# Due times of a list schedule shifted label by label, in a two-block transformer kernel

## Chip, cores and metric
One core of a Trainium2 chip runs the kernel. The metric is the device time of one execution in microseconds (us), the median of several runs; less is better.

## What is computed
Two transformer blocks, one behind the other, on 256 tokens of width 1024 in float32. The first puts 16 meta tokens in front, and has grouped-query attention (8 heads on 2 key and value heads, part A), differential attention (4 heads, two score maps each, part B), an output projection and a SwiGLU feed-forward of width 2816. The second has a gated spatial branch, a dilated window attention in three patterns, two gates, a merge through two branch matrices and an output matrix, and a squared-relu feed-forward of width 4096. In short:

```python
h = rms_norm(x, attn_norm_g)
proj = einsum('bld,de->ble', h, w_in)             # q, k, v of A and of B
out_a = softmax(qa ka^T * scale) va               # after norm and rope of q and k
out_b = rms_norm((p0 - lam * p1) vb) * 0.8        # p0, p1 = two softmaxes per head
x = x + concat(out_a, out_b) @ w_out
h = rms_norm(x, ffn_norm_g)
x = x + (silu(h @ w_gate) * (h @ w_up)) @ w_down
...
merged = g_a * (y_a @ w_branch_a) + g_b * (y_b @ w_branch_b)   # second block
h = h + rms_norm(merged @ w_out)
h = h + rms_norm(square(relu(rms_norm(h) @ w_up)) @ w_down)
```

## The kernel before
All weights come as 235 chunks of 128 x 1024 float32 through four raw buffers (wraw). Each chunk is split into a high part (whi, ScalarE rounds it to fp32r) and a low part (wlo, VectorE subtracts), into one of six pairs of buffers; a product is then the sum of three fp32r matmuls, high by high, high by low and low by high. Activations are held the same way (hx for the normed input, mix for what goes into output projections). Results come in eight PSUM banks, each read by ScalarE and VectorE before it is used again.

No engine call is issued where it stands in the code. A `Recorder` (line 235) takes each one down with its dependences, its price by a formula (`price`, line 308; a VectorE operation costs 68 + 1.042 ns per column, for one) and the label that is current then. The labels name stages: for the first block PqA0 to PvB3 (projections), K1 and K2 (norm of a key), Q1 (norm sums of a query), V1 (transposed values), SA and SB (scores and softmax), TA and TB (transposed probabilities), VA and VB (times the values), N1 and N2 (norm of B), WO (output projection), "sums" and "warm" at the start, gateA and upA (the first 512 columns of the feed-forward by tokens), lead and f4 to f21 (the rest of it in columns of 128); for the second block names with a quote: GV, GU, SP (spatial branch), AV (values), Pq and Pk (projections), S2, T2, V2 (attention), GT (gates), BR (the two branch products and their merge), and out2, mlp0, mlp1, lead2, m4 to m31, down2 without one. `transposed` adds t0 and t1 to a label for its two groups of transposes.

`flush` is called twice (lines 1152 and 1461): behind f6, and at the end. Each call turns the recorded operations into an order. It sets a target end for every matmul, takes the due time of every other operation back from those through prices and latencies, and runs a list scheduler (`schedule`, line 346) in which each engine, whenever it is free, takes what is ready in the plan and due first. It does that six times; each round's targets are the PE times of the round before, with BIAS, a fixed -3 us on twelve labels of transposes. The order with the least PE clock in the plan is issued. Operations of one score group (R.group) are kept together, and buffers and banks are given out when an operation is recorded, ahead of any order. SP issues all DMAs in the scheduled order too.

Of the kernel before, what the change touches and what calls it, by code (L numbers as in the profile page):

```python
# [29 lines left out]
class Plan:  # L30


    def __init__(self):
        self.tasks = {}
# [164 lines left out]
def _within(a, b):  # L199
# [13 lines left out]

LATE = {
    ("tensor", "scalar"): 240.0, ("tensor", "vector"): 250.0, ("tensor", "tensor"): 0.0,
    ("scalar", "tensor"): 280.0, ("scalar", "vector"): 145.0, ("scalar", "scalar"): 0.0, ("scalar", "gpsimd"): 220.0,
# [8 lines left out]
def late(a, b):  # L227
    return LAND if a == "sync" else LATE.get((a, b), 150.0)

# [5 lines left out]
class Recorder:  # L235


    def __init__(self, tc, nc):
        self.tc, self.nc = tc, nc
        self.ops, self.acc, self.label, self.next = [], {}, "", set()  # L240
        self.clock = {e: 0.0 for e in ("tensor", "vector", "scalar", "gpsimd", "sync")}

    def engine(self, name):
# [160 lines left out]
    def flush(self):  # L404
        ops = self.ops
        pe, target = self.clock["tensor"], []
        for o in ops:
            if o.eng == "tensor":
                pe += o.cost
            target.append(pe if o.eng == "tensor" else 1e18)  # L410
        best = None
        for _ in range(ROUNDS):
            target = [t + BIAS.get(o.label, 0.0) for t, o in zip(target, ops)]
            order, at, clock = self.schedule(target)
            if best is None or clock["tensor"] < best[2]["tensor"]:
                best = order, at, clock
            target = [at[o.i] + o.cost if o.eng == "tensor" else 1e18 for o in ops]
        order, at, self.clock = best
        for i in order:
            o = ops[i]  # L420
            o.at = at[i]
            o.fn(*o.args, **o.kw)  # L422
        self.ops, self.acc = [], {}
# [1198 lines left out]
```

## Time and profile before

| | us |
|---|---|
| median of 3 runs | 739.33 (738.82 to 739.93) |
| the profiled execution's own time | 738.85 |
| its span, first to last instruction | 737.1 |
| PE (TensorE matmul) busy | 723.6 |
| DVE (VectorE) busy | 539.0 |
| ACT (ScalarE) busy | 431.3 |
| POOL (GpSimd) busy | 67.9 |

PE stands for matmuls, PEld for the loads of their stationary operand, SP for the queue that issues DMAs. All instructions carry line 422, the one that issues the plan's order, so groups are told apart by tiles: `out<-in`. A wait is the idle time ahead of an instruction on its own engine, with the instruction that ended it. A float32 matmul of full precision (norm sums, transposes of two columns) is recorded twice.

### The profile page before, as it was taken

The numbers are of one execution on the slowest core, as the hardware profiler recorded it, in microseconds if no ns is written. First come the engines' busy times: TensorE is split into PE (matmuls) and PEld (weight loads), VectorE is DVE, ScalarE is ACT, GpSimd is POOL, SyncE is SP. The second block draws the span as 40 slices with busy tenths as digits, with TensorE's granted clock in tenths as the row PEclk, the third lists the DMA queues.
The fourth block names the chain that finished last, engine by engine and source line by source line (L and its number), as shares of the span: only waits on it lengthen the run. The fifth ranks groups of instructions, "written<-read, shape, count | busy, mean of one in ns | idle before, by whom it ended". The sixth has DMA issues, their size and how long they took to land.

```text
span 737.1 us, 11095 instructions
## 1 busy us (share of the span) xinstructions
PE 723.6 (98%) x4085; PEld 625.3 (85%) x4085; DVE 539.0 (73%) x944; ACT 431.3 (59%) x779; POOL 67.9 (9%) x81
## 2 busy tenths in 40 slices
PE   8989999999999999999999999999999999999996
PEld 5989988888888888888888889888888888888885
DVE  6897986666666665678748999757999766666663
ACT  6697775655555545466646766656656544454441
POOL 5932230100000000010000000000130000000000
PEclk8999999999999999999999999999999999999998
DMA  8553314466865565547655444545646755555621
GB/s 286 166 194 122 136 58 144 143 204 229 296 197 182 191 196 195 181 142 255 215 187 177 157 153 138 171 159 191 194 149 192 251 190 195 194 190 189 197 89 57
DMA packets 37639, 131.85 MB, mean 179 GB/s; under 512 B 4432, under 2 KB 5200, under 8 KB 37584
## 3 DMA queue, kind: packets, MB, share of 16 engines
q1 hardware_dynamic: 37584, 131.14, 53.8%
q8 instruction: 32, 0.52, 0.3%
q14 instruction: 23, 0.19, 0.1%
HBM read 130.07 MB, written 1.05 MB: 178 GB/s over the span
## 4 chain that ended last, share of the span: by engine, by line
PE 89%; DVE 5%; ACT 3%; issue 1%; DMA 1%; SPq 0%; POOLq 0%; POOL 0%; DVEq 0%; ACTq 0%
PE bank L422 89%; DVE wlo L422 2%; ACT prob L422 1%; DVE tiny L422 1%; DMA prob<-in_xT_dram 1%; ACT whi L422 1%; DVE ro L422 0%; DVE ptl L422 0%; DVE qkf L422 0%; DVE rr L422 0%; ACT hx L422 0%; DVE q L422 0%; ACT L422 0%; ACT vhiA L422 0%; SPq L422 0%
## 5 line engine op out<-in xcount | busy, mean ns | idle before, releaser
L422 DVE TENSOR_TENSOR wlo<-wraw,whi 128x1024 fp32r<-128x1024 f32 (+1 forms) x235 | 286.9, 1225 | 117.6 <-ACT whi L422 115.6
L422 ACT ACTIVATE whi<-wraw 128x1024 fp32r<-128x1024 f32 (+1 forms) x235 | 245.3, 1052 | 126.9 <-issue 73.4
L422 PE MATMUL bank<-hx,whi 128*128 128x512 f32 (+2 forms) x1152 | 270.2, 370 | 3.7 <-DVE ptl L422 1.1
L422 PEld LDWEIGHTS bank<-hx,whi 128*128 128x128 f32 x1152 | 196.2, 190 | 34.8 <-ACT whi L422 1.9
L422 PE MATMUL bank<-whi,mix 128*128 128x512 f32 x496 | 154.9, 392 | 0.0
L422 PEld LDWEIGHTS bank<-hx,wlo 128*128 128x128 f32 x1008 | 136.7, 189 | 9.5
L422 PE MATMUL bank<-hx,wlo 128*128 128x256 f32 (+1 forms) x1008 | 141.8, 283 | 0.0
L422 PEld LDWEIGHTS bank<-whi,mix 128*128 128x128 f32 x496 | 92.9, 188 | 17.1
L422 PE MATMUL bank<-wlo,mix 128*128 128x512 f32 x248 | 96.2, 391 | 0.0
L422 PE MATMUL bank<-whi,hx 128*128 128x512 f32 x288 | 91.6, 397 | 0.0
L422 PEld LDWEIGHTS bank<-whi,hx 128*128 128x128 f32 x288 | 54.0, 188 | 12.2
L422 PE MATMUL bank<-wlo,hx 128*128 128x512 f32 x144 | 56.2, 396 | 0.0
L422 PEld LDWEIGHTS bank<-wlo,mix 128*128 128x128 f32 x248 | 46.6, 188 | 9.2
L422 ACT ACTIVATE scr<-bank 128x256 f32<-128x256 f32 x64 | 24.0, 375 | 48.8 <-PE bank L422 48.7
L422 POOL TENSOR_TENSOR tiny<-tiny,half 128x1 f32<-128x1 f32 (+1 forms) x15 | 14.8, 989 | 405.5 <-DVE tiny L422 405.2
L422 DVE TENSOR_TENSOR scr<-bank,scr 128x256 f32<-128x256 f32 x64 | 27.0, 422 | 26.5 <-ACT scr L422 26.5
L422 PEld LDWEIGHTS bank<-wlo,hx 128*128 128x128 f32 x144 | 27.1, 188 | 6.4 <-DVE wlo L422 0.4
L422 ACT ACTIVATE prob<-bank,tiny,rq 128x272 f32<-128x272 f32 x32 | 18.1, 575 | 10.1 <-DVE tiny L422 10.1
L422 POOL TENSOR_TENSOR gates<-xres,gains 128x1024 f32<-128x1024 f32 x2 | 5.0, 2506 | 193.7 <-ACT hx L422 180.8
L422 PE MATMUL bank<-mix,whi 128*128 128x512 f32 x64 | 21.6, 397 | 0.0
L422 ACT ACTIVATE qkf<-bank 128x256 f32<-128x256 f32 x28 | 10.5, 376 | 17.6 <-PE bank L422 17.5
L422 DVE TENSOR_TENSOR mix<-scr,mix 128x256 fp32r<-128x256 f32 x46 | 19.3, 419 | 0.5 <-ACT mix L422 0.5
(213 smaller groups left out, 706.1 us busy)
## 6 DMA issues: line engine op xcount, KB each, us to landing
wraw<-in_w_dram SPq DMA_DIRECT2D x233, 512.0 KB, 3.4
prob<-in_xT_dram SPq DMA_DIRECT2D x4, 272.0 KB, 4.7
xres<-in_x_dram SPq DMA_DIRECT2D x2, 512.0 KB, 4.4
rope<-in_rope_dram SPq DMA_DIRECT2D x1, 544.0 KB, 7.8
wraw<-in_w_dram SPq DMA_DIRECT2D x2, 256.0 KB, 4.3
gains<-in_ffn_norm_g_dram SPq DMA_DIRECT2D x1, 512.0 KB, 4.2
gains<-in_norm_mix_pre_dram SPq DMA_DIRECT2D x1, 512.0 KB, 4.6
qkf<-in_ln_dram SPq DMA_DIRECT2D x1, 512.0 KB, 5.2
```

Source lines behind the costliest of these rows:

```text
L422: o.fn(*o.args, **o.kw)
```

## The change
A table SHIFT holds two dictionaries, for the first and the second flush, from labels to nanoseconds. After the six rounds, `flush` runs the scheduler once more. Its targets are those from which the best round was scheduled, each plus the shift of its operation's label (0 for a label without an entry). The new order is taken if its PE clock in the plan is less than the best round's. The numbers were found by a search that ran the same scheduler. The program's operations, prices, buffers and BIAS stay as they are.

```diff
+SHIFT = (
+    {"VB3": 2112, "N2B1": -4655, "TB1": -4647, "PqA3": -3128, "sums": -115, "PvB2": -5273, "N1B3": 8204,
+     "K1B2": 21917, "warm": -8619, "TB0": -15908, "K1B1": 9384, "PqA0": 22008, "TA1": -4031, "N1B1": 9789,
...
+     "N1B0": 7205, "PvA": 10889, "N2B0": 20402, "K2B2": 3528, "PkB1": 7584, "WO7": -8494, "K1B3": 3058,
+     "f6": -3059, "Q1A2": 8170, "PqB0": -4696, "Q1A3": -3057, "VB2": 19, "WO2": 14517, "PkB2": 3071,
...
+     "Q1A1": 25254, "WO1": -7596, "TA0": 2190, "SB0": 10775, "K2B3": 5218, "SA2": -9475, "PqB3": -4295,
+     "VB0": 10705, "upA1": 2965, "Q1B0": 53238, "SB3": -5790, "PvB0": -1187, "f5": -3031, "PvB3": 9694,
+     "gateA0t1": -9585, "PkB3": -3237, "PkA": -22491, "lead1": 7921, "TA3": -17310, "WO0": 2469, "f4": 11559,
...
+     "PkB0": 2335, "TA2": -12748, "V1A": 26377, "Q1B1": 1421, "V1B0": -5710, "PqB2": 4158, "K1A": -5300,
+     "gateA1t0": 12011, "PqA1": 4415, "SA0": 9077},
+    {"f7": 3307, "Pk01'": -453, "T2_2'": 1212, "mlp1t0": -1952, "mlp0t1": -1518, "GT1'": -2969, "AV0'": 2363,
+     "V2_0'": 604, "Pq20'": -3811, "Pq10'": 890, "BR7'": 4155, "mlp0t0": 628, "BR5'": 6508, "BR1'": 5154,
+     "GT10'": 8835, "BR2'": 4471, "GT15'": 2439, "f17": 7795, "GT4'": -6113, "Pk10'": -2668, "m20": -825,
+     "m4": 6142, "S2_0'": -732, "GT9'": -6294, "f18": -745, "f8": -377, "GV1't1": -1193, "out2": -3606,
+     "lead21": -961, "GT6'": 1850, "m14": 2598, "BR4'": -110, "m30": -1200, "Pq11'": -828, "Pk20'": -4908,
...
+     "m15": 1585, "GT5'": 2381, "S2_1'": 3635, "GT14'": -3451, "GT3'": 11952, "m31": 968, "m10": -3776,
...
+     "f12": 334, "Pk02'": 2934, "m18": 3994, "Pk00'": -108, "Pq23'": 598, "mlp1": 2034, "GT8'": 746,
+     "f9": 10621, "GT0'": 399, "BR6'": 585, "m26": 5665, "m11": 5565, "m19": -582, "m28": 3496, "AV1'": 443,
+     "S2_2'": -733, "m22": 417, "GV0't1": -2959, "lead20": 13132, "BR0'": 4917, "mlp1t1": -1864,
+     "GU3'": 3771, "T2_1'": 638, "down": 244, "m21": 906, "down2": 11687, "Pk03'": 664, "Pk23'": 8163,
...
+)
...
-        self.ops, self.acc, self.label, self.next = [], {}, "", set()
+        self.ops, self.acc, self.label, self.next, self.part = [], {}, "", set(), 0
...
             if best is None or clock["tensor"] < best[2]["tensor"]:
-                best = order, at, clock
+                best, base = (order, at, clock), target
             target = [at[o.i] + o.cost if o.eng == "tensor" else 1e18 for o in ops]
+        part, self.part = SHIFT[self.part], self.part + 1
+        best = min(best, self.schedule([t + part.get(o.label, 0) for t, o in zip(base, ops)]), key=lambda b: b[2]["tensor"])
         order, at, self.clock = best
```

## Rows read from the trace of the kernel before

**Rows 1.** The page: the span, each engine's busy time (share of the span, instructions), and PE's granted clock in 40 equal slices, in tenths.

```profile
span 737.1 us, 11095 instructions
...
PE 723.6 (98%) x4085; PEld 625.3 (85%) x4085; DVE 539.0 (73%) x944; ACT 431.3 (59%) x779; POOL 67.9 (9%) x81
...
PEclk8999999999999999999999999999999999999998
```

**Rows 2.** Windows by stage: the stretch, its length, busy us of PE, PEld, DVE, ACT and POOL with their instructions, granted clock, DMA share, GB/s.

```profile
30.00:55.00 25.00, 22.88 (x194) 21.14 (x195) 24.42 (x61) 21.12 (x53) 13.14 (x14) 1.00 0.49 169
...
100.00:420.00 320.00, 320.00 (x1700) 273.48 (x1699) 222.31 (x348) 187.29 (x312) 9.13 (x11) 1.00 0.57 189
...
424.00:731.00 307.00, 306.75 (x1637) 263.35 (x1636) 227.43 (x363) 167.39 (x288) 9.94 (x6) 1.00 0.53 172
```

**Rows 3.** Waits of PE over the whole span: the tile it was to write, what ended the wait, us in total, times, longest. (The single waits for prob, qkr, sq and vloA stand in rows 4.)

```profile
PE bank L422 <- DVE half L422: 1.2, 1, 1.2
PE bank L422 <- DVE ptl L422: 1.1, 2, 0.6
PE bank L422 <- ACT whi L422: 1.0, 1, 1.0
...
PE bank L422 <- DVE hx L422: 0.6, 2, 0.3
...
PE bank L422 <- ACT hx L422: 0.5, 1, 0.5
...
```

**Rows 4.** Timeline of PE, the lines with a wait behind 11.35 us: start, us, operation, and in brackets the idle time before and what ended it.

```profile
29.90 0.39 PE L422 MATMUL bank<-hx,whi 128*128 128x256 f32 x1 [0.25 <-DVE vloA L422]
...
39.23 1.79 PE L422 MATMUL bank<-ident,prob 128*128 128x128 f32 x10 [0.96 <-ACT prob L422]
...
43.14 2.15 PE L422 MATMUL bank<-hx,whi 128*128 128x256 f32 x16 [0.61 <-DVE ptl L422]
...
54.63 2.28 PE L422 MATMUL bank<-hx,whi 128*128 128x272 f32 x16 [0.46 <-DVE ptl L422]
...
76.37 0.83 PE L422 MATMUL bank<-ind,sq 128*128 128x2 f32 x6 [0.49 <-ACT sq L422]
...
422.01 0.50 PE L422 MATMUL bank<-qkr 128*128 128x256 f32 x2 [0.63 <-DVE qkr L422]
```

**Rows 5.** The three longest pieces of the chain of work that ended last (start, us, what, count), and from the timeline of PE its last matmul.

```profile
99.67 307.96 PE bank L422 x1622
...
422.01 133.58 PE bank L422 x768
...
555.59 169.73 PE bank L422 x859
...
730.36 0.39 PE L422 MATMUL bank<-wlo,mix 128*128 128x512 f32 x1
```

**Rows 6.** Timeline of ScalarE and VectorE in the start, 5 to 12.5 us.

```profile
6.62 0.43 ACT L422 ACTIVATE gains<-prob 128x272 f32<-128x272 f32 x1 [0.47 <-DMA prob<-in_xT_dram]
6.96 0.92 ACT L422 ACTIVATE hx<-prob,cols 128x272 fp32r<-128x272 f32 x2
...
8.43 0.69 DVE L422 TENSOR_TENSOR wlo<-wraw,whi 128x512 fp32r<-128x512 f32 x1
9.04 2.25 DVE L422 SCALAR_TENSOR_TENSOR hx<-prob,cols,hx 128x272 fp32r<-128x272 f32 x4
```

**Rows 7.** The branch merge: windows of 20 us from 520 on; groups of VectorE from 500 to 560 us (count, busy us, mean ns of one, idle before); a product of GpSimd on the gates (min/median/max ns, first and last start); and from the timeline of PE the first matmul of the merge and the first behind it.

```profile
520.00:540.00 20.00, 20.00 (x101) 16.77 (x100) 19.97 (x33) 10.01 (x19) 6.09 (x3) 1.00 0.55 173
540.00:560.00 20.00, 20.00 (x95) 16.07 (x94) 19.80 (x27) 12.48 (x23) 3.31 (x3) 1.00 0.48 158
...
L422 DVE TENSOR_TENSOR wlo<-wraw,whi 128x1024 fp32r<-128x1024 f32 x19 | 23.1, 1219 | 3.1 <-ACT whi L422 3.1
...
L422 DVE TENSOR_TENSOR tmp<-bank,tmp 128x256 f32<-128x256 f32 x16 | 6.4, 415 | 0.0
...
L422 DVE SCALAR_TENSOR_TENSOR hx<-tmp,hx 128x256 fp32r<-128x256 f32 x8 | 3.3, 416 | 0.0
...
L422 DVE SCALAR_TENSOR_TENSOR tmp<-gates,tmp x16: 412/420/2634, 509.9 to 538.4; 128x256 f32<-128x256 f32 x16
...
L422 DVE TENSOR_TENSOR tmp<-tmp,tmp x8: 413/418/2615, 512.6 to 539.9; 128x256 f32<-128x256 f32 x8
...
L422 POOL TENSOR_TENSOR gates<-xres,gains x2: 2390/2506/2622, 520.3 to 535.8; 128x1024 f32<-128x1024 f32 x2
...
506.74 0.39 PE L422 MATMUL bank<-mix,whi 128*128 128x512 f32 x1
...
529.24 0.62 PE L422 MATMUL bank<-whi,hx 128*128 128x512 f32 x2
```

**Rows 8.** Timeline of PE: the end of the first score group with the matmul behind it, and two matmuls of 512 columns in the output projection.

```profile
34.10 0.29 PE L422 MATMUL bank<-kloA,q 64*128 64x272 f32 x2
34.23 0.29 PE L422 MATMUL bank<-khiA,q 64*128 64x272 f32 x2
34.45 0.50 PE L422 MATMUL bank<-hx,wlo 128*128 128x256 f32 x2
...
109.70 0.40 PE L422 MATMUL bank<-whi,mix 128*128 128x512 f32 x1
109.93 0.39 PE L422 MATMUL bank<-wlo,mix 128*128 128x512 f32 x1
```

14 rows, old and new, of the table SHIFT are left out of this document.

## Prediction

> **What bounds the kernel now.** I read the page first [rows 1]: TensorE (PE) is busy for 723.6 of 737.1 us and the granted clock is full in all but the first and last slices. So 13.5 us are all that an order of work can win back, and the next question is where they lie. The view of waits [rows 3, 4] names 4.4 + 2.3 = 6.7 us of them. Another 6.3 us lie behind the last matmul, which ends at 730.75 [rows 5]; that is the closing chain of ScalarE, VectorE, GpSimd and the output's DMA. The remaining 0.5 us are scraps.
>
> The windows [rows 2] then split the named waits by stage. From 100 to 420 us and from 424 to 731 us PE is busy in all but 0.25 us of 627, and those 0.25 lie behind its last matmul. The chain [rows 5] says the same: three PE pieces of 308, 134 and 170 us with no other engine between. So a microsecond saved ahead of 100 us comes out at the end in full, since nothing later has slack to take it back, and no reordering among the two feed-forward loops (labels f7 to f21 and m4 to m31) can gain anything. The gain has to come from the attention stage, 11 to 80 us, and from one place at 421 us.
>
> Is a busy PE a PE at its pace? The 512-column pair in [rows 8] starts 0.23 us apart, about 2.2 columns per ns at the full clock of 2.4 GHz, so there is little slack inside "busy". The Trainium skill, Perfetto Trace Analysis, section "Identifying the Most-Contended Engine", says that matmul busy time is a poor measure of distance from the roofline and that the weight-load share should be read instead. That share is 85% from 100 to 420 us [rows 2], so by the page there would be 46 us of room there; the even starts speak against it (rival 4).
>
> **The change part by part.** The change adds no instruction, wait or DMA to the program. It schedules once more, with the due times of the best of the six rounds plus one number per label, and takes that order if the planner's own PE clock then ends earlier. What moves is the order in each engine's queue, SP's DMA issues and GpSimd's queue included; buffers, banks and their order of reuse are fixed when the operations are recorded. The list scheduler never leaves an engine idle on purpose: it takes, of what the plan thinks is ready, the one due first. So a shift matters only where two ready operations compete.
>
> The six waits behind the start [rows 4], with what the table does to the label at the head of the queue (labels by the list order and the shapes):
> - 0.96 us at 39.23: the transposes of TA0 wait for the softmax. TA0 is pushed 2.2 us later, about the time of most of a projection (24 matmuls, 3 us), which can go in front. Gone: 0.96.
> - 0.49 at 76.37: a key norm's sums (K1B2, six short matmuls) wait for ScalarE's squares. Pushed 21.9 later. Gone: 0.49.
> - 0.63 at 422.01: scores of S2_1 wait for VectorE's split of q or k. Pushed 3.6 later. Gone: 0.63.
> - 0.46 at 54.63: a projection (PkB1) waits for a bank that VectorE's ptl copy holds. Pushed 7.6 later. Gone: 0.46.
> - 0.61 at 43.14: the same wait for PqB0, which is pulled 4.7 earlier. Kept.
> - 0.25 at 29.90: PqA3 waits for the bank of V1A. PqA3 is pulled 3.1 earlier, V1A pushed 26 later; the two pull against each other. Kept.
>
> Sum that goes: 0.96 + 0.49 + 0.63 + 0.46 = 2.54 us; kept 0.86. That the table pushes just those labels back which head the queue in a wait speaks for the plan having seen these waits, so that they aren't only errors of its prices.
>
> What it costs: an order that is tight in the plan waits on the chip wherever a duration is longer than planned, and the stage has no reserve on VectorE, which is busy for 24.42 of 25 us from 30 to 55 [rows 2]. The plan prices a 1024-column VectorE split at 68 + 1.042 x 1024 = 1135 ns and the trace has 1219 [rows 7]. The trace of before cannot show the new waits. Their bounds are none and as many as now, six of 3.40 / 6 = 0.57 us. I take two, 1.14 us: four places are cleared and perhaps half of them come back elsewhere.
>
> The start: ScalarE runs a square of the token sums (gains, 0.43 us) ahead of two splits of hx, and PE waits 0.54 us for that hx [rows 3, 6]; later VectorE's hx makes it wait 0.34 and 0.31. PkA is pulled 22 us earlier, so its splits outrank the sums. Bounds 0 and 0.43 + 0.34 = 0.77 us; but the x blocks arrive late anyway and VectorE does a 0.69 us wlo ahead of four hx splits [rows 6] with both of them serving PkA, so I take 0.1.
>
> Score groups: their 64-row matmuls follow each other 0.13 us apart in pairs, while the next 128-row one starts 0.22 behind the last pair [rows 8], so leaving the mode costs some 0.09 us. The Trainium skill, TensorEngine Tiling (Array Packing), section "Key Properties", says that changing the tiling mode drains the engine; the trace agrees, at that 0.09 us. The group is recorded as one unit, so their number stays but for two halves of SB3 that could become neighbours: 0 to 0.2 us, taken as nothing.
>
> Second flush apart from S2_1: PE has no wait there, so nothing to gain; the cost bounds are nothing and rival 3. The tail behind the last matmul keeps its order, since all of down2 carries one shift (+11.7 us) and was last already: 0. Weight loads: no wait of PE is put down to a DMA [rows 3, 4], and DMA share is 0.57 or less in the long stretches [rows 2]; earlier or later issue costs 0.
>
> Sum: -2.54 + 1.14 - 0.10 = -1.5 us. The profiled execution took 738.85 us, 1.75 of them outside its span of 737.1, so it would become 737.35. The median of before is 739.33, 0.48 above that execution; the same step from it gives 737.8.
>
> **The rivals.**
> 1. Waits move, their sum stays. For it: all six waits come from VectorE or ScalarE running later than planned, in a stage where VectorE is full [rows 2, 4]; another order has other places with the same errors. Against it: four labels are moved in just the direction that clears them. Time: -0.6 to +0.6, so 739.3. The case that the new pass isn't taken at all, or hardly differs, falls here too (0).
> 2. The whole gain. No new waits and the start improves: -2.54 - 0.77 = -3.3 us, 736.0; with all six gone -4.2, 735.1. For it: after 80 us the present order already shows that PE can run for 300 us without a wait. Against it: VectorE's 24.42 of 25 us.
> 3. Slower: the branch merge (labels BR0 to BR7). VectorE is busy 19.97 and 19.80 us in the two 20 us windows from 520 on [rows 7]. One BR takes it 2 x 0.415 + 2 x 0.42 + 0.418 + 0.416 + 1.219 = 3.7 us, and single ones of them last 2.6 instead of 0.42 us, beside GpSimd's 2.5 us products on gates (the maxima of their rows). PE needs 22.5 us for the eight BRs and shows no wait only because out2 steps cover VectorE's lateness. The table pushes the BRs back by 3.2 us on average (BR5 6.5, BR3 0) and pulls out2 3.6 ahead. If the last merge comes 3.2 us later and out2 has no other matmul to run, PE waits up to 3.2: with the -1.5 that is +1.7, 741.0, and +3.2 if part one brings nothing. It decides from 3.0 us uncovered, since 1.5 are eaten by the gain and 1.5 more make a slower kernel. Against it: real dependencies, not due times, set when VectorE can merge, and the pushes are of one sign, so the eight keep most of their order.
> 4. A busy PE hides slack that a better order would use. The weight-load share of 85% [rows 2] would leave up to 320.0 - 273.5 = 46.5 us from 100 to 420 us, 693 if all were won there. Against it: starts every 0.23 us in [rows 8], which no order of the queue can bring closer, and a change that acts on waits only.
>
> **How the numbers follow.** A difference of 0.2%, 1.5 us, is about what a measurement of this kernel tells from none. Forecast (-2.4 to -0.6, centre -1.5): 0.45. Rival 1: 0.23. Rival 2: 0.17. Rival 3: 0.14. Rival 4: 0.01. The forecast sits on the bound, so half of it counts as faster: 0.22 + 0.17 + 0.01 = 0.40 faster; 0.23 + 0.23 = 0.46 same; 0.14 slower. Predicted time 737.8. The range reaches to most of rival 2 at the low end and to a part of rival 3 at the upper: 735.6 to 740.4; the forecast's own range is 736.9 to 738.7.
>
> **What the profile will show.** Right: PE's named waits after 11 us fall from 3.4 to about 2 us, the transposes of TA0 and the scores of S2_1 have a projection right ahead of them, PE stays full from 100 us to the end, and the time between the last matmul and the end of the span stays 6.3 us. The last matmul ends near 729.2 instead of 730.75. Wrong: PE waits of 0.5 us and more at new places in 30 to 80 us with a sum of 3 us or over (rival 1), none at all (rival 2), or a PE wait for VectorE's hx or tmp between 510 and 560 us (rival 3). A tail longer than 6.3 us, or a wait for a DMA, would be something I have not seen.

## The result and the profile after

The changed kernel takes 748.61 us (median of four runs, 747.68 to 748.93) where the kernel before took 739.25 beside it: a ratio of 1.0127, 95% interval [1.0114, 1.014]. It is 9.4 us slower; the forecast was 1.5 us faster, and 748.6 lies beyond the upper end of the range, 740.4. One execution of e1_first (below), which took 1842.8 us, is left out of its median; with it that would be 740.58.

The page of the profiled execution (748.44 us):

```profile
span 746.7 us, 11053 instructions
...
PE 729.0 (98%) x4085; PEld 625.4 (84%) x4085; DVE 532.1 (71%) x944; ACT 433.1 (58%) x779; POOL 71.8 (10%) x81
...
PEclk8999999999999999999999999999999999999999
```

Against [rows 1] the span grew by 9.6 us with the same 4085 matmuls, and PE's busy time by 5.4. VectorE is busy 7 us less and ScalarE 2 us more; the work is the same. More than half of the loss lies inside the rows that say "busy", and it has to be looked for there. Little of it can be waiting: a matmul of 512 columns is recorded with 0.39 us while the next starts 0.23 us behind it [rows 8], so the first 0.16 us of a wait count as busy, and no more.

The waits of PE over the whole span (the tile it was to write, what ended the wait, us in total, times, longest), to be held against [rows 3]:

```profile
PE bank L462 <- ACT whi L462: 3.3, 2, 1.7
PE bank L462 <- ACT hx L462: 2.1, 2, 1.1
PE bank L462 <- DVE hx L462: 1.3, 1, 1.3
...
PE bank L462 <- POOL gains L462: 0.6, 1, 0.6
PE bank L462 <- DVE prob L462: 0.5, 1, 0.5
...
```

And from PE's timeline the places (as in [rows 4]; start, us, operation, count, in brackets the idle time before), with the last matmul:

```profile
22.52 0.38 PE L462 MATMUL bank<-ones,gains 128*128 128x2 f32 x2 [0.59 <-POOL gains L462]
...
38.06 0.44 PE L462 MATMUL bank<-ident,prob 128*128 128x128 f32 x2 [0.29 <-ACT prob L462]
...
42.58 1.79 PE L462 MATMUL bank<-hx,whi 128*128 128x256 f32 x13 [0.49 <-DVE ptl L462]
...
83.63 0.55 PE L462 MATMUL bank<-ident,prob 128*128 128x128 f32 x3 [0.53 <-DVE prob L462]
...
142.12 0.50 PE L462 MATMUL bank<-whi,hx 128*128 128x512 f32 x1 [1.01 <-ACT hx L462]
...
206.25 0.50 PE L462 MATMUL bank<-hx,whi 128*128 128x512 f32 x1 [1.56 <-ACT whi L462]
...
548.72 0.50 PE L462 MATMUL bank<-whi,hx 128*128 128x512 f32 x1 [1.06 <-ACT hx L462]
...
550.76 0.79 PE L462 MATMUL bank<-whi,hx 128*128 128x512 f32 x1 [1.32 <-DVE hx L462]
...
551.78 1.05 PE L462 MATMUL bank<-whi,hx 128*128 128x512 f32 x2
...
554.12 0.62 PE L462 MATMUL bank<-whi,hx 128*128 128x512 f32 x2
...
739.95 0.39 PE L462 MATMUL bank<-wlo,mix 128*128 128x512 f32 x1
```

The four waits that were to go are gone or small (TA0 0.29 of 0.96). Four waits of over 1 us stand where the kernel before had none: at 142, 206, 549 and 551 us. The last matmul ends at 740.34 instead of 730.75.

The loss can be booked from two numbers of each trace. Up to its last matmul PE is idle for what its busy time leaves: 730.75 - 723.61 = 7.14 us before, 740.34 - 728.98 = 11.36 after, so +4.2 us of idle time and +5.4 us of busy time. By place: the first flush of the schedule (to 183 us) ends its last matmul at 183.19 instead of 182.86, and the second takes 557.2 instead of 547.9 us. The planner's own PE clock said 173.73 and 717.89 at the end of the two flushes, where the plan before said 177.14 and 721.86. It promised 4.0 us.

**The wait at 142 us.** ScalarE's timeline there, and the two places ahead of the wait at 206 us:

```profile
139.07 0.60 ACT L462 ACTIVATE hx<-bank 128x512 fp32r<-128x512 f32 x1 [4.25 <-PE bank L462]
139.69 1.28 ACT L462 ACT_TABLE_LOAD   x1
140.98 0.60 ACT L462 ACTIVATE prob<-bank 128x512 f32<-128x512 f32 x1
141.47 0.59 ACT L462 ACTIVATE hx<-bank 128x512 fp32r<-128x512 f32 x1
...
192.00 1.06 ACT L462 ACTIVATE whi<-wraw 128x1024 fp32r<-128x1024 f32 x1 [4.37 <-DMA wraw<-in_w_dram]
...
205.14 1.06 ACT L462 ACTIVATE whi<-wraw 128x1024 fp32r<-128x1024 f32 x1 [1.32 <-DMA wraw<-in_w_dram]
```

The gate matmuls of the second half (gateA1) need both copies to hx. The table pushes one of the two transposes, gateA1t0, 12 us later, so that a Silu of the first half (prob) gets between the copies. The Silu brings 1.28 us of loading ScalarE's function table, a step that the plan has no price for. Before, both copies ran at 139.5 and the load behind them.

**The wait at 206 us.** A matmul of f11 waits for ScalarE's copy of a weight (whi), and ScalarE waits for the weight's DMA, twice in this stretch. The table pushes f9 10.6 us later and pulls f11 6.4 us earlier, and SP's queue issues what is due first: in the plan's order a load recorded under f10 goes ahead of the last one under f9, and so does a copy of ScalarE. Before, f8 to f11 follow one another.

**The merge of the branches.** VectorE's timeline and GpSimd's, one behind the other:

```profile
542.76 3.19 DVE L462 TENSOR_TENSOR wlo<-wraw,whi 128x1024 fp32r<-128x1024 f32 x1 [0.15 <-ACT whi L462]
545.88 0.41 DVE L462 TENSOR_TENSOR tmp<-bank,tmp 128x256 f32<-128x256 f32 x1
...
548.70 2.01 DVE L462 SCALAR_TENSOR_TENSOR hx<-tmp,hx 128x256 fp32r<-128x256 f32 x1 [0.48 <-ACT hx L462]
...
542.35 2.52 POOL L462 TENSOR_TENSOR gates<-gates,gains 128x1024 f32<-128x1024 f32 x1 [11.05 <-DVE tmp L462]
547.89 2.54 POOL L462 TENSOR_TENSOR gates<-xres,gains 128x1024 f32<-128x1024 f32 x1 [3.02 <-issue]
```

A split (wlo) that takes 1.22 us in [rows 7] takes 3.19, and a merge of 0.42 takes 2.01. Each ends about where a product of GpSimd has ended and its own time has passed: 542.35 + 2.52 + 1.22 = 546.1 (ends 545.95), 547.89 + 2.54 + 0.42 = 550.9 (ends 550.71). The step in between, at 545.88 with no product of GpSimd beside it, takes its 0.41. Before, such holds fell on steps that PE had other matmuls to cover; now the last merge ends at 550.7 and PE has nothing else. The Trainium skill, SBUF — State Buffer, section "SBUF: two separate sides", says that VectorE and GpSimd take turns on one pair of ports, held for a whole instruction, when a VectorE step reads two tensors from that memory. The trace agrees, at the 3.19 and 2.01 us.

**The clock.** Windows of the two places (busy us of PE, PEld, DVE, ACT and POOL, granted clock, DMA share, GB/s):

```profile
200.00:210.00 10.00, 8.44 (x46) 6.94 (x45) 5.79 (x8) 4.32 (x8) 0.00 (x0) 1.00 0.77 258
...
540.00:560.00 20.00, 17.62 (x73) 13.50 (x73) 16.09 (x22) 8.71 (x15) 5.59 (x3) 0.91 0.41 133
```

From 550.4 us, near the end of the second wait, the granted clock is at the lower of its two levels, 1.2 GHz, for 3.41 us. In the timeline above two matmuls take 1.05 us together at 551.78, and two take 0.62 at 554.12, where the clock is full again. Before, the clock was full through the merge [rows 7]. This stretch lies inside "busy".

The other three and a half us of busy time have no one place. Most of them are matmuls whose starts lie a little farther apart: from one 512-column matmul of the second flush to the next start it is 229.3 ns in the mean before and 230.7 after (starts over 252 ns apart, which are waits, and the slow stretch left out), and there are some 1800 of them.

### The profile page after: what moved, and what is told of

Its sections match the earlier page's. It is cut to its first block, busy times and chain, and to the rows that moved or that the text cites. A ratio compares the mean times of both kernels' runs of the same rounds, so it can differ in the third digit from the quotient of the medians.

```text
span 746.7 us, 11053 instructions
## 1 busy us (share of the span) xinstructions
PE 729.0 (98%) x4085; PEld 625.4 (84%) x4085; DVE 532.1 (71%) x944; ACT 433.1 (58%) x779; POOL 71.8 (10%) x81
## 3 DMA queue, kind: packets, MB, share of 16 engines
HBM read 130.07 MB, written 1.05 MB: 176 GB/s over the span
## 4 chain that ended last, share of the span: by engine, by line
PE 72%; ACT 2%; DVE 2%; DMA 2%; issue 2%; POOLq 0%; POOL 0%; DVEq 0%; ACTq 0%
PE bank L462 72%; DMA wraw<-in_w_dram 2%; ACT whi L462 1%; DVE wlo L462 1%; DVE hx L462 0%; ACT gat L462 0%; ACT qkf L462 0%; ACT prob L462 0%; DVE tiny L462 0%; DVE scr L462 0%; DVE prob L462 0%; DVE tmp L462 0%; ACT hx L462 0%; ACT qkr L462 0%; ACT junk L462 0%
## 5 line engine op out<-in xcount | busy, mean ns | idle before, releaser
L462 PE MATMUL bank<-hx,whi 128*128 128x512 f32 (+2 forms) x1152 | 300.6, 372 | 4.6 <-ACT whi L462 3.3
L462 PEld LDWEIGHTS bank<-hx,whi 128*128 128x128 f32 x1152 | 199.3, 190 | 35.4 <-ACT whi L462 4.8
L462 PE MATMUL bank<-hx,wlo 128*128 128x256 f32 (+1 forms) x1008 | 172.6, 284 | 0.0
L462 PEld LDWEIGHTS bank<-hx,wlo 128*128 128x128 f32 x1008 | 154.2, 189 | 12.8 <-issue 0.3
L462 PE MATMUL bank<-whi,hx 128*128 128x512 f32 x288 | 93.9, 403 | 3.4 <-ACT hx L462 2.1
L462 PE MATMUL bank<-wlo,mix 128*128 128x512 f32 x248 | 90.0, 393 | 0.0
L462 ACT ACTIVATE mix<-scr 128x256 fp32r<-128x256 f32 x46 | 18.7, 413 | 17.1 <-DVE scr L462 17.1
L462 POOL TENSOR_TENSOR gates<-xres,gains 128x1024 f32<-128x1024 f32 x2 | 7.8, 3890 | 187.0 <-ACT whi L462 183.9
L462 ACT ACTIVATE prob<-prob,tiny 128x272 f32<-128x272 f32 (+1 forms) x32 | 17.2, 567 | 7.0 <-DVE tiny L462 7.0
```

## The experiments

Kernels with a changed table take the order of the shifted pass in any case, so that what runs is the table and not the choice between two plans. The matmuls, the arithmetic and the buffers are those of the changed kernel, but for e3_no_lock. "Changes of bank" are counted in the plan's PE queue: a matmul that follows one into another bank. There are 278 + 460 in the two flushes before, 547 + 1537 after.

What the runs and their traces gave (idle: end of the last matmul less busy time):

| kernel | median us | ratio to before, 95% | last matmul ends | PE busy | PE idle | clock at its lower level between 16 us and the last matmul |
|---|---|---|---|---|---|---|
| before | 739.25 | | 730.75 | 723.61 | 7.14 | no |
| after | 748.61 | 1.0127 [1.0114, 1.014] | 740.34 | 728.98 | 11.36 | 3.41 us at 550 |
| e1_first | 740.27 | 1.002 [1.001, 1.0029] | 731.32 | 723.73 | 7.59 | no |
| e2_second | 747.42 | 1.0108 [1.0091, 1.0125] | 739.89 | 728.88 | 11.01 | 3.41 us at 550 |
| e3_no_lock | 745.41 | 1.0105 [1.0066, 1.0143] | 736.92 | 727.17 | 9.75 | no |
| e5_pairs | 741.47 | 1.0028 [1.0016, 1.0041] | 733.67 | 726.05 | 7.62 | no |
| e4_no_loops | 747.67 | 1.0115 [1.01, 1.013] | 739.45 | 727.62 | 11.83 | 3.41 us at 322 |
| e7_no_merge | 750.86 | 1.015 [1.0116, 1.0184] | 744.58 | 733.55 | 11.03 | 3.41 at 24, 6.83 at 41, 3.41 at 570 |
| e9_first_keep | 738.87 | 1.0 [0.9987, 1.0013] | 730.59 | 723.87 | 6.72 | no |
| e12_f9_f11 | 747.72 | 1.0106 [1.0087, 1.0126] | 740.53 | 729.59 | 10.94 | 3.41 us at 551 |
| e10_priced | 737.5 | 0.9981 [0.9971, 0.999] | 728.78 | 724.27 | 4.51 | no |
| e11_priced2 | 736.2 | 0.996 [0.9948, 0.9971] | 728.09 | 724.06 | 4.03 | no |

Theory: the plan leaves out four things, and the table, searched with this plan, moves work to where they cost most: the hold between VectorE and GpSimd, the load of a function table, the late weights, and the price of alternating between banks. Rival: one cause, or the mere fact that the order has no slack left.

### Half of the table: e1_first and e2_second

```diff
+SHIFT = (SHIFT[0], {})      # e1_first
+SHIFT = ({}, SHIFT[1])      # e2_second
```

> The first dictionary alone, the second one emptied, so that the second flush has the order of before. The plan's PE clock ends 3.4 us earlier than that of before. In the trace of the changed kernel the first flush's last matmul ends at 183.19 us, in that of before at 182.86. Theory (the loss of 9.4 us comes from the second dictionary, and the first only fails to bring its planned 3.4 us): 739.3 to 740.3 us. Rival (the tight order of the attention stage is what the rest pays for, by weights that come late behind it): 743 us or more, with a PE wait for weights at 200 to 210 us.

> The second dictionary alone, the first one emptied, so that the first flush has the order of before. The plan's PE clock ends 0.6 us earlier than that of before. Theory (the second dictionary costs it all): 747.5 to 749 us, with the two PE waits for hx near 548 us, a fall of the granted clock behind them, and a wait for weights near 205 us. Rival (both dictionaries are needed): 742 to 745 us.

The halves cost 1.2 and 8.3 us against the runs of before beside them (739.09), and 9.5 together, where the whole table costs 9.4: they add up. The first lies at the upper end of what the theory gave it (its runs spread from 739.1 to 742.1, and the profiled one took 739.44), the second 0.1 below its lower end. The first half keeps the wait at 142 us (1.02 us there) and its promised gain of 3.4 us is not to be seen. In the second, the two waits of the merge and the fall of the clock stand, and the late weights with them, but at another place:

```profile
274.85 1.19 PE L468 MATMUL bank<-hx,whi 128*128 128x512 f32 x4 [1.04 <-ACT whi L468]
...
548.05 0.50 PE L468 MATMUL bank<-whi,hx 128*128 128x512 f32 x1 [1.05 <-ACT hx L468]
...
550.11 0.51 PE L468 MATMUL bank<-whi,hx 128*128 128x512 f32 x1 [1.32 <-DVE hx L468]
```

### The hold alone: e3_no_lock

```diff
+            if o.eng == "gpsimd" and o.label == "BR7'":
+                o.args = [x[:, :8] for x in o.args]
```

> The changed kernel in its own order, but GpSimd's three products on the gates take 8 of their 1024 columns; the rest of those products is left out. In the changed kernel VectorE's operations beside them last 2.44, 3.19 and 2.01 us instead of 1.21, 1.21 and 0.41, 4.8 us in sum, PE then waits 1.06 and 1.32 us for the last merges, and the granted clock is half for 3.4 us. Theory (GpSimd's products hold VectorE up, which makes the last merge late and lets the clock fall): both waits and the fall go, 4 us less: 744 to 745.3 us. Rival (the merges are late by their due times alone): the waits stay above 1.5 us in sum and the time at 747 us or more.

The order is the changed kernel's, and only GpSimd's products are short. VectorE's split and GpSimd's second product in the same merge:

```profile
543.79 1.23 DVE L464 TENSOR_TENSOR wlo<-wraw,whi 128x1024 fp32r<-128x1024 f32 x1
...
534.31 0.32 POOL L464 TENSOR_TENSOR gates<-gates,gains 128x8 f32<-128x8 f32 x1 [14.17 <-DVE tmp L464]
```

It takes 745.41 us, just above the upper end of what the theory gave. Both waits of PE are gone, the clock stays full, and the last matmul ends 3.42 us earlier: 1.61 less idle, 1.81 less busy. So the hold made those waits, and the 1.81 us is about what the slow stretch cost. The two waits were 2.38 us; 0.7 of that came back in late weights (1.89 at 206.8 instead of 1.56, and 0.38 at 277). In the rest of the trace 727.17 - 723.61 = 3.56 us of busy time stay above that of before, at a full clock. That is the part without one place.

### Alternation alone: e5_pairs

```diff
+SHIFT = ({}, {f"f{f}": -5500 for f in range(9, 20, 2)}
+             | {f"m{f}": -5500 for f in range(5, 30, 2)})
```

> The kernel before with its first order, and in the second flush only the odd labels f9 to f19 and m5 to m29 are due 5.5 us earlier, taken in any case. The plan's PE clock doesn't move (721.86 us), but the plan's PE queue changes its bank 1320 times in the second flush instead of 460. Theory (a 512-column matmul that changes the bank starts the next one 3 to 4 ns later, which no wait shows): 860 x 3.5 ns = 3.0 us more, 741.5 to 743.5 us, with no named PE wait in the two loops. Rival (a change of bank is free): 738.8 to 739.8 us.

The order of before, but in both loops every second label comes due earlier, so that it shares the queue with the one ahead of it. The plan's clock doesn't move. The kernel loses 2.4 us (739.09 beside it), the lower end of what the theory gave, and PE's idle time rises by only 0.5. Its window from 555 us to the end:

```profile
555.00:740.00 185.00, 178.46 (x893) 150.18 (x891) 118.78 (x179) 84.57 (x137) 1.63 (x3) 0.99 0.53 174
```

The same window of before has 175.75 busy us: 2.7 more matmul time lies behind 555 us, since the work arrives there later and then goes slower. In the trace as a whole busy time is up by 726.05 - 723.61 = 2.44 us for 860 more changes of bank, 2.8 ns each. The starts say the same: the mean distance behind a 512-column matmul of the second flush grows from 229.3 to 230.6 ns, 2.3 us over some 1800 of them. Alternating two streams of matmuls has a price, then.

For the 1077 more changes in the changed kernel's second flush 2.8 ns each would be 3.0 us; by the starts in e3_no_lock (230.8 ns) it is 2.7. The 269 more in the first flush cost next to nothing: the busy time of e1_first, which has them all, is 0.12 us above that of before. So some 0.8 of the 3.56 us that e3_no_lock leaves is something else. Waits would fit, though that isn't shown: it has 11 of them behind 11 us where the kernel before has 6, with up to 0.16 us of each inside "busy".

What in the alternation costs, the other bank, the other weights or the other moving tensor, isn't told apart, and not every change costs. In the loops of the second flush wlo of mix and then whi of mix into another bank start 226.5 ns apart, before and in e5_pairs alike. Behind whi with hx the next of the same kind starts 228.2 ns later in the same bank and 231.9 in another before (346 and 15 of them), 228.3 and 233.3 in e5_pairs (93 and 268).

### Without the loops, without the merge: e4_no_loops and e7_no_merge

```diff
+SHIFT = (SHIFT[0], {n: v for n, v in SHIFT[1].items()
+                    if not (n[0] in 'fm' and n[1:].isdigit())})            # e4_no_loops
+SHIFT = (SHIFT[0], {n: v for n, v in SHIFT[1].items()
+                    if n[:2] not in ('BR', 'GT') and n != 'out2'})         # e7_no_merge
```

> The changed kernel without the shifts of the labels f and m (the 512-column matmuls of the two loops); every other shift stays. Theory (alternation of the two matmul streams costs some 2.8 ns for each added change, as the run e5_pairs showed, and the late weight transfer at 206 us comes from the shifts of f9 and f11): 535 fewer changes give back 1.5 us and the weight wait of 1.6 us is gone, so about 745.5 us (744.5 to 746.5) where the changed kernel takes 748.6; the two waits in the merge near 549 us and the fall of the granted clock behind them stay. Rival (the loops' order costs nothing by itself, the 4 us are in the sums and the merge): 747 us or more, with the weight wait gone or moved.

> The changed kernel without the shifts of the labels BR, GT and out2 in the second dictionary (the branch merge and the last output's matmuls keep the due times of the kernel before). Theory (the merge of the branches, pushed later, stands beside GpSimd's products with nothing left for TensorE to do): no wait over 0.5 us between 540 and 556 us, the granted clock full to the end, and 744.5 to 745.8 us where the changed kernel takes 748.6. Rival (the products of GpSimd hold VectorE wherever the merge is put, since the rest of the second table brings the work together): waits of 1 us or more stay between 530 and 556 us and the time is 747.5 us or more.

By the times both rivals won, and the theory's sum was wrong in both; the traces say why. In e4_no_loops the late weights at 206 us are gone, and a new wait for ScalarE's hx stands at 321:

```profile
321.44 0.50 PE L468 MATMUL bank<-whi,hx 128*128 128x512 f32 x1 [2.04 <-ACT hx L468]
```

Behind it the clock falls for 3.41 us, while behind the waits of the merge, which are there as before (1.07 and 1.33 us), it now stays full. So one wait and one fall were exchanged for another of each. Busy time is lower than after's by 1.36 us, with one fall of the same length in both. That is about the price of alternation that was expected, 1.5 us. The expectation on the pace held; the one on the waits didn't.

In e7_no_merge no wait is left between 540 and 560 us and the clock is full there, as the theory had it. Instead:

```profile
209.12 0.50 PE L468 MATMUL bank<-hx,whi 128*128 128x512 f32 x1 [1.53 <-ACT whi L468]
...
280.75 1.19 PE L468 MATMUL bank<-hx,whi 128*128 128x512 f32 x4 [1.77 <-ACT whi L468]
...
568.97 1.32 PE L468 MATMUL bank<-ident,scr 128*128 128x128 f32 x8 [1.63 <-DVE scr L468]
```

The last of them, again with a fall of the clock behind it, is the next step in line, transposes that wait for VectorE behind the merge. The runs spread from 747.26 to 752.68, and the profiled one is the slowest; its clock was also at the lower level for 10.2 us between 24 and 48 us. Its median is no measure of the merge. What its trace shows is that the merge has no wait without the shifts of BR, GT and out2.

### The table load: e9_first_keep

```diff
+SHIFT = ({n: v for n, v in SHIFT[0].items() if not n.startswith('gateA')}, {})
```

> The first dictionary alone, without the shifts of the label gateA; the second is empty. Beside it stands e1_first (the first dictionary whole: 740.58 us), which had a wait of 1.02 us at 142.29 us because ScalarE loaded the table for Silu between the two copies that the gate matmuls wait for. Theory (the load of the table, which the plan doesn't price, makes that wait): both copies go ahead of the load, the wait is gone, and 739.2 to 740.0 us come out, although the plan itself ends 0.84 us later than that of e1_first. Rival (the plan is right about this place): 741 to 742 us.

```profile
138.84 1.27 ACT L468 ACTIVATE hx<-bank 128x512 fp32r<-128x512 f32 x2 [3.97 <-PE bank L468]
140.13 1.28 ACT L468 ACT_TABLE_LOAD   x1
```

Both copies go ahead of the load and the wait of 1 us is gone; a shorter one for hx, 0.53 us, stands at 133. The kernel takes 738.87 us, 1.4 less than e1_first, although its plan ends 0.84 us later; the intervals of the two ratios touch, so the time alone says little. By the trace the plan has this place the wrong way round, for want of the load's 1.28 us. What is left of the first half neither gains nor loses: a ratio of 1.0 [0.9987, 1.0013], where the plan still promised 2.6 us.

### Two labels of the first loop: e12_f9_f11

```diff
+SHIFT = (SHIFT[0], {n: v for n, v in SHIFT[1].items() if n not in ('f9', 'f11')})
```

> The changed kernel without the shifts of two labels of the first loop alone, f9 (+10.6 us) and f11 (-6.4 us); the plan ends at 717.89 us as before them, with 77 changes of bank fewer. Theory (these two shifts put the issue of f10's and f11's weights ahead of f9's, and the wait of 1.56 us for ScalarE's copy of a late weight at 206 us comes from that): the wait near 206 us is gone and 746.8 to 747.4 us come out, where the changed kernel takes 748.6. Rival (the weights come late whatever the order of f9 and f11, since the whole loop draws on the transfers sooner): a wait of over 1 us on a weight between 195 and 290 us stays and the time is 748 us or more.

The wait at 206 us is gone, so it needs the swap of f9 and f11. The swap alone doesn't set the place: e2_second has it too, and its late weights come at 275. About half of the wait came back further on in the same loop, and the time, 747.72, lies between theory and rival; its interval overlaps that of the changed kernel:

```profile
275.79 0.73 PE L468 MATMUL bank<-hx,whi 128*128 128x512 f32 x2 [0.82 <-ACT whi L468]
```

### A table searched with the missing prices: e10_priced and e11_priced2

```diff
+SHIFT = (
+    {... 64 labels ...},
+    {... 51 labels ...},
+)                            # e10_priced; e11_priced2: 65 and 49 labels
```

> A new table in the place of the old one (64 and 51 labels). It was searched not with the plan's own end but with the end of the plan's queues run in order with prices that the runs before this one showed: 2.8 ns for each 512-column matmul that follows one into another bank, 1.28 us for each change of ScalarE's function table, some 60 ns added to each hand-over between engines, matmuls at twice their price in the first 10.2 us, and VectorE and GpSimd not at once in their long products. Its plan ends at 718.83 us, 0.94 us later than the plan of the changed kernel (717.89), with 874 changes of bank where that one has 2084. Theory (the shifts of the due times can help, and the changed kernel lost because its table was searched without these prices): faster than the kernel before by 2 to 4 us, 735 to 737.5 us, with no wait of TensorE over 0.8 us behind 11 us. Rival (any order searched to leave the plan no slack meets other delays on the chip, whatever the prices): 738.5 us or more, with new waits of 1 us.

> A second table of the same search from another start (65 and 49 labels; its plan ends at 719.11 us, 882 changes of bank). Theory: as e10_priced, 735 to 737.5 us. Rival: 738.5 us or more. If the one gains and the other does not, the prices are too coarse to rely on.

Both are a little faster than the kernel before: 737.5 us, at the upper end of what was expected (its runs lie at 736.6 to 737.5 and at 738.6 to 739.1, and the profiled one took 736.88), and 736.2, ratio 0.996 [0.9948, 0.9971], so that the better one wins 0.4%. Two of the prices are settings of the search that no run here measures by themselves: the 60 ns, and the start, where the trace of before has the clock at its lower level for 6.83 us, not 10.2. For e11_priced2, its page, its remaining waits over 0.2 us behind 11.1 us with its last matmul from PE's timeline, and its GpSimd:

```profile
span 734.4 us, 11091 instructions
...
PE 724.1 (99%) x4085; PEld 625.6 (85%) x4085; DVE 533.6 (73%) x944; ACT 432.2 (59%) x779; POOL 74.5 (10%) x81
...
```

```profile
41.37 2.16 PE L468 MATMUL bank<-hx,whi 128*128 128x256 f32 x16 [0.31 <-DVE ptl L468]
50.98 0.89 PE L468 MATMUL bank<-hx,whi 128*128 128x272 f32 x5 [0.22 <-DVE ptl L468]
62.73 0.55 PE L468 MATMUL bank<-ident,rw 128*128 128x128 f32 x3 [0.22 <-POOL rw L468]
...
727.71 0.39 PE L468 MATMUL bank<-wlo,mix 128*128 128x512 f32 x1
```

```profile
518.02 3.77 POOL L468 TENSOR_TENSOR gates<-xres,gains 128x1024 f32<-128x1024 f32 x1 [180.62 <-issue]
531.90 8.07 POOL L468 TENSOR_TENSOR gates<-gates,gains 128x1024 f32<-128x1024 f32 x1 [10.12 <-DVE tmp L468]
```

The waits behind the start are down to a few tenths, and the hold now falls on GpSimd, whose product of some 2.5 us takes 8.07 with nobody waiting for it. Idle time falls by 3.1 us against before and busy time rises by 0.45, all of it in the first flush; behind it the 512-column matmuls start 229.3 ns apart, as before. The plan of this order ends at 719.11, 1.2 us later than that of the changed kernel, and on the chip it is 12.4 us faster: by the plan's own clock the search was led the wrong way.

## Why the prediction was wrong

**What held.** The bound was read rightly: idle time in the attention stage and at 421 us was what an order could win, and e11_priced2 leaves PE 3.1 us less idle, most of it in just those places (named waits behind 11 us: 0.75 instead of 3.40). The four waits that were to clear did so (0.67, 0.49, 0.63 and 0.46 us, 2.25 where 2.54 was forecast), the two that were to stay stayed, the named waits of the start fell by 0.5 us instead of 0.1 (those for hx by 1.2, while the one for the first whi grew from 1.02 to 1.70), and the closing chain kept its 6.3 us.

**The step that failed** is the one that gave the second flush nothing: "PE has no wait there, so nothing to gain; the cost bounds are nothing and rival 3", with "earlier or later issue costs 0" for the weights, and, ahead of it, that nothing could be gained by reordering the two loops. That a full PE can gain nothing was right. That it can lose nothing didn't follow: it was full because this order had slack at each hand-over, and the table spends it. The second half of the table costs 8.3 of the 9.4 us (e2_second). Term by term:

- New waits. The sum took two of 0.57 us; there are nine, 6.8 us together. Those below 100 us are 0.59, 0.53, 0.24 and 0.21, near what was taken for one (0.57). The big four, 5.0 us, are each something that the plan doesn't price, and each went in an experiment of its own: the merge (2.4 us) in e3_no_lock, the late weights (1.56, half of which came back) in e12_f9_f11, the table load (1.0) in e9_first_keep. The average of the old waits was no measure for them: an old wait is a price that is off by some tenths, a new one is a whole step without a price.
- Rival 3 named the right place and mechanism for the largest of them, VectorE's merge beside GpSimd's products with out2 as no cover. It asked for 3.0 us uncovered and priced itself at 741.0. The waits were 2.4 us, short of its point; but a fall of the clock came behind them and cost some 1.8 more, which was in no term. With 4.2 us it would have ended the forecast alone.
- The pace of a busy PE. Rival 4 asked whether busy time hides slack, and the even starts spoke against a gain; that it could be lost was not asked. Some 2.7 us of the 9.6 went that way, 1.5 ns at each 512-column matmul of the second flush (e3_no_lock; e5_pairs has it by alternation alone, and e4_no_loops gives part of it back). In [rows 8] the price can't be read: it is one hundredth of a matmul's 0.23 us.
- The argument that the table pushes just those labels which wait, so that "the plan has seen these waits", held for the waits and misled for the whole: the plan also moved labels where it saw no cost and the chip has one.

Idle +4.2, clock 1.8 and the other 3.6 us of busy time (2.7 of them pace) make 9.6, the shift of the last matmul.

**What the single runs can't carry.** Undoing a part gave back less than its waits each time (e4_no_loops, e7_no_merge, e12_f9_f11): the next unpriced hand-over stood behind it. So the terms add up in one trace but not across kernels. That the order lost by its prices, and not merely by having no slack, rests on e10_priced and e11_priced2: they leave PE less idle than any other order here and are faster. Their plans end some 1 us later than that of the changed kernel, though, and a search that ends as late without these prices was not run; that the prices made the difference is likely but not shown.

**Open:** what in the alternation of two streams costs; why the clock fell behind some waits of 1 to 2 us and not behind others; and which of the prices in the last search mattered most.

## What to carry to other kernels

A queue order searched on a plan is only as good as the prices that the plan leaves out: look in the trace for table loads, for steps of VectorE that stretch beside GpSimd, and for weights that land late, and price them before the search. Here two tables searched with such prices gained 0.2 and 0.4%. An engine that is full in the trace can still be slowed by an order, so for each stretch without waits ask what covers each hand-over now, not only what it could gain. When a change clears the waits it aimed at and still loses, hold busy time against busy time first; what grew there is mostly pace or clock, and no view of waits shows it.

## What the hardware showed unexpectedly

- Matmuls of the two loops that alternate between streams cost 2.8 ns more per change of bank, at full clock and with hardly a wait more in the trace: 2.44 us for 860 changes in e5_pairs. The price isn't even: none behind wlo with mix, 5 ns behind whi with hx.
- The granted clock fell to its lower level for 3.41 us behind waits of 1.06 and 1.32 us two us apart (after, e2_second, e12_f9_f11), behind one of 2.04 (e4_no_loops) and one of 1.63 (e7_no_merge); it didn't behind 1.89 us (e3_no_lock), 1.77 (e7_no_merge, at 281 us) or the 1.07 and 1.33 of e4_no_loops. Behind the merge it cost some 1.8 us on top of the waits' 2.4 (e3_no_lock).
- The hold between VectorE and GpSimd goes both ways: 1.22 us of VectorE became 3.19 in the changed kernel, and 2.5 us of GpSimd became 8.07 in e11_priced2.
